# Seven products instead of eight in both MLP matrix products, by 2x2 blocks

## The chip, the cores and the metric

One core of a Trainium2 chip runs the whole program. The metric is the device time of the program in microseconds (us). TensorE (PE) multiplies, VectorE (DVE), ScalarE (ACT) and GpSimd (POOL) do the element-wise work, SyncE (SP) issues nearly all DMAs. Each engine takes its instructions in order and waits on semaphores.

## The reference

A trunk of one layer on 1024 tokens of 1024 channels, in fp32: an adaLN-conditioned mixer with four branches, gates and an output projection, and then the MLP that this change is about.

```python
def reference(x, c, positions, norm1_g, norm2_g, ada_w, ada_b, w_in, ..., w_out, mlp_w1, mlp_w2, final_g):
    ...
        h = rmsnorm(x, norm2_g[l]) * (1.0 + scale2) + shift2
        x = x + gate2 * (jnp.square(jax.nn.relu(h @ mlp_w1[l])) @ mlp_w2[l])
    return rmsnorm(x, final_g)
```

`mlp_w1` is 1024 x 4096, `mlp_w2` 4096 x 1024. `rmsnorm` divides by the root of the mean square over the channels.

## The kernel before

Activations lie transposed, channels on the 128 partitions and tokens along the free axis, in two halves of 512 tokens (`hf` 0 and 1). Each fp32 product is made of three: `split` (L109, L110) casts a matrix to `hi` on ACT and subtracts on DVE, `lo = raw - hi`; `mm3` (L125) issues hi·hi, hi·lo and lo·hi as matmuls of 128x128 by 128x512 into one PSUM bank. Weights come as blocks `raw` of 512 KB and are split as they arrive.

`outproj` makes `x1` half by half: eight channel blocks, each 24 matmuls, the residual on DVE (L1039), the square on ACT and the sum of squares `ssq`. `rstd` sums `ssq` over the partitions with a matmul by ones (`one`, L1065), takes the root on ACT (L185) and four reciprocals on DVE (L187). `norm_block` (L175 to L177) then makes `gh`, `gl`, the split input of the MLP.

`mlp` runs over 16 groups of 256 hidden channels. In a group, `up` makes four blocks (two channel blocks, two halves) of 24 matmuls each, applies relu on ACT (L1094) and the square on DVE (L1095), and splits the result into `aa`; `down` multiplies it into all eight output blocks, six matmuls each, and adds each to `x1` on DVE (L1107). Hidden activations and `x1` stay in SBUF. The first up products need the first half's norm only. The last two groups are written out in another order, with the last quarter in 256-column pieces, so that the final norm (L1119 to L1122) of earlier tokens is made beside the matmuls of later ones.

A scheduler orders the recorded program for each engine; pools (`wp`, `bp`, `pb`) decide which tiles share memory, and so some of the waits.

Of the kernel before, what the change touches and what calls it, by code (L numbers as in the profile page):

```python
# [9 lines left out]
FP32 = mybir.dt.float32  # L10
FR = mybir.dt.float32r
# [4 lines left out]
P = 128  # L16
# [47 lines left out]
def layout(x, c, positions, norm1_g, norm2_g, ada_w, ada_b, w_in, dn_conv_w, dn_a_log,  # L64
# [19 lines left out]
    o["w2"] = ct(A["mlp_w2"][0].reshape(32, P, 1024))  # L84
# [13 lines left out]
class Trunk:  # L98
# [45 lines left out]
    def cond_rows(self, pool):  # L144
        """Silu of the condition, the same row on all partitions."""
# [43 lines left out]
    def start(self):  # L189
        nc, A = self.nc, self.A  # L190
        cp = self.cp
        self.cst = cp.tile([P, NCST], FP32, name="cst")
# [251 lines left out]
    def rsqrt(self, x, y, t):  # L444
        """y = x ** -0.5 by Newton's iteration."""
# [17 lines left out]
    def dn_scalars(self):  # L463
        """Generator: beta, the decays and their logs per token, [token, head, chunk]."""
# [31 lines left out]
    def dn_proj(self, s, h):  # L496
        """Projection s of q, k, v of head h: its generator, the taps on DVE, the Silu."""
# [55 lines left out]
    def dn_mix(self, h, q, kT, vT, Es):  # L553
# [61 lines left out]
        # the 32-blocks on the diagonal for the inverse: partition = column group * 32 + block * 8 + chunk  # L615
# [8 lines left out]
    def dn_inverse(self, s):  # L624
        """Generator: the inverses of the 32-blocks by substitution, then back to the blocks' places."""
# [28 lines left out]
    def dn_levels(self, s):  # L654
        """The inverse of the 128-blocks out of that of the 32-blocks, doubled twice; transposed in TT."""
# [22 lines left out]
    def dn_scan(self, h, s):  # L678
# [44 lines left out]
        # rms norm with the norm of q folded in  # L723
# [129 lines left out]
    def mixers(self):  # L853
        """DeltaNet and retention: the projections of later heads fill the waits of the chains."""
# [83 lines left out]
    def branches(self, order, ahead=3):  # L938
        nc, A, bp = self.nc, self.A, self.pb
        blk = lambda w, n, o=0: [w[:, (o + k) * P:(o + k + 1) * P] for k in range(n)]  # L940
        self.acc = [bp.tile([P, NB, 512], FP32, tag="acc", name="acc", bufs=2) for _ in range(2)]
# [7 lines left out]
        def load_y(br):  # L949
            yh = bp.tile([P, 4, T], FR, tag="y", name="yh", bufs=2)  # L950
            yl = bp.tile([P, 4, T], FR, tag="y", name="yl", bufs=2)
# [65 lines left out]
    def outproj(self):  # L1017
# [5 lines left out]
        self.x1, self.gh, self.gl = [None] * 2, [None] * 2, [None] * 2  # L1023
        rs = [None, None]

        def h2(hf, k):
            self.norm_block(self.x1[hf][:, k], rs[hf], self.a2[:, k:k + 1], self.modc[:, 24 + k:25 + k],
                            self.gh[hf][:, k], self.gl[hf][:, k], bp, "t2k", 4)
        for hf in range(2):
            x1 = self.x1[hf] = bp.tile([P, NB, 512], FP32, tag="acc", name="x1", bufs=2)  # L1030
            ssq = bp.tile([P, 512], FP32, tag="ssq", name="ssq", bufs=1)
            for db in range(NB):
# [7 lines left out]
                                               op0=ALU.mult, op1=ALU.add)  # L1040
                self.sumsq(x1[:, db], ssq, db, nc.vector if db == NB - 1 else nc.gpsimd)
                if hf == 1 and db > 0:
                    h2(0, db - 1)
            if hf == 1:
                h2(0, NB - 1)
# [25 lines left out]
    def mlp(self):  # L1071
        nc, A, bp = self.nc, self.A, self.pb
        blk = lambda w: [w[:, k * P:(k + 1) * P] for k in range(NB)]
        NG = 16

        def load2(g):
            w2 = []
            for fb in range(2):
                raw = self.wp.tile([P, 1024], FP32, tag="raw", name="raw", bufs=2)
                nc.sync.dma_start(out=raw, in_=A["w2"][2 * g + fb])  # L1080
                bh = bp.tile([P, 1024], FR, tag="bh", name="bh", bufs=2)
                bl = bp.tile([P, 1024], FR, tag="bl", name="bl", bufs=2)
                self.split(raw, bh, bl)
                w2.append((bh, bl))
            return w2

        def up(aa, w, fb, hf, o=0, n=512):
            wh, wl = w
            sl = slice(hf * 512 + o, hf * 512 + o + n)
            ps = self.psm()[:, :n]  # L1090
            self.mm3(ps, blk(wh), blk(wl), [self.gh[hf][:, k, o:o + n] for k in range(NB)],
# [137 lines left out]
```

## Time and profile before

| | before |
|---|---|
| runs | 2035.49, 2041.83, 2037.52 us |
| median | 2037.52 us |
| profiled execution: span | 2034.8 us |
| TensorE busy | 1972.2 us, 97% |
| DVE, ACT, POOL busy | 54%, 28%, 9% |
| mean granted clock of TensorE | 0.993 |

The span is that of one profiled execution, from its first to its last instruction; the median of the runs is 2.7 us longer. Busy shares are means over stages that differ much, so the stage of the change has windows of its own below.

### The profile page before, as it was taken

The page shows a single profiled execution, that of the slowest core. Times are in us where ns is not written, and L with a number is a line of the kernel's source. Part 1 is how long each engine was busy: PE and PEld are TensorE (multiplying, and loading weights), DVE is VectorE, ACT ScalarE, POOL GpSimd, SP SyncE. Part 2 cuts the span into 40 slices and gives each one's busy share as a digit, 9 for nine tenths or more (in the row PEclk, how much of TensorE's full clock was granted, in tenths as well). Part 3 has the DMA queues.
Part 4 walks back from the last instruction along what each step waited for, and adds up shares of the span by engine and source line. Part 5 has one row for each costly group of instructions (what it writes and reads, how often), then busy time and mean ns, then how long its engine had stood idle before and what let it go on. Part 6 is the DMA issues. An engine that isn't in the chain of part 4 may idle for free.

```text
span 2034.8 us, 23666 instructions
## 1 busy us (share of the span) xinstructions
PE 1972.2 (97%) x9460; PEld 1629.6 (80%) x9460; DVE 1096.4 (54%) x1947; ACT 566.6 (28%) x922; POOL 187.6 (9%) x151
## 2 busy tenths in 40 slices
PE   5999989999999999999999999999999999999997
PEld 3888867777888888788788788878888888888886
DVE  7755679776744461352522224774455544455567
ACT  4524534332212231211212123432211222211133
POOL 4101211010000000011111112200000000000001
PEclk9999999999999999999999999999999999999999
DMA  7322121132222271251511213321111111111122
GB/s 280 128 84 84 54 54 43 43 75 72 63 73 63 78 237 48 92 167 52 163 55 45 90 42 104 124 73 46 48 52 42 42 63 51 43 52 42 42 83 93
DMA packets 89178, 162.10 MB, mean 80 GB/s; under 512 B 39014, under 2 KB 41702, under 8 KB 89068
## 3 DMA queue, kind: packets, MB, share of 16 engines
q1 hardware_dynamic: 87788, 156.40, 23.8%
q0 software_dynamic: 1280, 4.20, 0.9%
q8 instruction: 74, 1.21, 0.3%
q14 instruction: 36, 0.29, 0.0%
HBM read 142.20 MB, written 14.17 MB: 77 GB/s over the span
## 4 chain that ended last, share of the span: by engine, by line
PE 56%; DVE 1%; DMA 0%; ACT 0%; issue 0%; DVEq 0%; ACTq 0%
PE mm L125 55%; DMA yraw<-yd 0%; DVE x L1122 0%; DVE rs L187 0%; DVE yl L110 0%; PE sm L1065 0%; ACT whi L109 0%; DVE nt L175 0%; DVE x L1107 0%; DVE sig L996 0%; ACT rs L185 0%; ACT yh L109 0%; DVE ssq L1060 0%; DVE bl L110 0%; ACT sig L970 0%
## 5 line engine op out<-in xcount | busy, mean ns | idle before, releaser
L125 PE MATMUL mm<-aa,bh 128*128 128x512 f32 (+1 forms) x1056 | 317.3, 383 | 0.0
L110 DVE TENSOR_TENSOR wlo<-raw,whi 128x1024 fp32r<-128x1024 f32 x121 | 151.3, 1251 | 283.1 <-ACT whi L109 282.4
L1107 DVE SCALAR_TENSOR_TENSOR x<-mm,modc,x 128x512 f32<-128x512 f32 (+1 forms) x264 | 192.1, 734 | 109.8 <-PE mm L125 107.9
L109 ACT CAST whi<-raw 128x1024 fp32r<-128x1024 f32 x123 | 129.2, 1051 | 423.4 <-PE mm L125 293.5
L125 PEld LDWEIGHTS mm<-aa,bh 128*128 128x128 f32 x1056 | 196.2, 188 | 39.0 <-DVE aa L110 0.3
L125 PE MATMUL mm<-hh,whi 128*128 128x512 f32 x560 | 218.3, 390 | 0.0
L125 PE MATMUL mm<-hh,wlo 128*128 128x512 f32 x560 | 218.0, 389 | 0.0
L125 PE MATMUL mm<-hl,whi 128*128 128x512 f32 x560 | 217.9, 389 | 0.0
L415 PE MATMUL mm<-hh,wlo 128*128 128x512 f32 x512 | 205.7, 402 | 0.0
L415 PE MATMUL mm<-hh,whi 128*128 128x512 f32 x512 | 205.5, 401 | 0.0
L415 PE MATMUL mm<-hl,whi 128*128 128x512 f32 x512 | 204.5, 399 | 0.0
L125 PE MATMUL mm<-aa,bl 128*128 128x512 f32 (+1 forms) x528 | 202.0, 383 | 0.0
L125 PE MATMUL mm<-gh,whi 128*128 128x512 f32 (+1 forms) x520 | 201.2, 388 | 0.0
L125 PE MATMUL mm<-gl,whi 128*128 128x512 f32 (+1 forms) x520 | 200.7, 386 | 0.5 <-DVE gl L177 0.5
L125 PE MATMUL mm<-gh,wlo 128*128 128x512 f32 (+1 forms) x520 | 200.6, 386 | 0.0
L109 ACT CAST bh<-raw 128x1024 fp32r<-128x1024 f32 x50 | 51.0, 1049 | 282.3 <-PE mm L125 275.3
L125 PEld LDWEIGHTS mm<-hh,whi 128*128 128x128 f32 x560 | 105.1, 188 | 22.4 <-issue 0.8
L125 PEld LDWEIGHTS mm<-hh,wlo 128*128 128x128 f32 x560 | 105.1, 188 | 22.0
L125 PEld LDWEIGHTS mm<-hl,whi 128*128 128x128 f32 x560 | 105.1, 188 | 21.5
L125 PEld LDWEIGHTS mm<-aa,bl 128*128 128x128 f32 x528 | 99.2, 188 | 19.3
L125 PEld LDWEIGHTS mm<-gl,whi 128*128 128x128 f32 x520 | 97.7, 188 | 21.1 <-DVE gl L177 0.9
L125 PEld LDWEIGHTS mm<-gh,whi 128*128 128x128 f32 x520 | 97.6, 188 | 20.4 <-issue 0.5
(308 smaller groups left out, 3154.6 us busy)
## 6 DMA issues: line engine op xcount, KB each, us to landing
raw<-in_wt SPq DMA_DIRECT2D x80, 512.0 KB, 3.5
raw<-in_w SPq DMA_DIRECT2D x69, 512.0 KB, 4.3
adaw<-in_ada SPq DMA_DIRECT2D x64, 256.0 KB, 3.9
adaw<-in_ada SPq DMA_DIRECT2D x16, 512.0 KB, 7.0
raw<-in_wbr SPq DMA_DIRECT2D x16, 512.0 KB, 4.0
yraw<-yd SPq DMA_DIRECT2D x32, 256.0 KB, 3.3
raw<-in_wo SPq DMA_DIRECT2D x16, 512.0 KB, 3.7
xt<-in_xT SPq DMA_DIRECT2D x16, 256.0 KB, 4.8
```

Source lines behind the costliest of these rows:

```text
L109: nc.scalar.copy(out=hi, in_=raw)
L110: (eng or nc.vector).tensor_tensor(out=lo, in0=raw, in1=hi.bitcast(FP32), op=ALU.subtract)
L125: self.nc.tensor.matmul(out=ps, lhsT=a, rhs=b, start=(i == 0), stop=(i == 3 * n - 1))
L415: self.nc.tensor.matmul(out=ps, lhsT=blk(a, k), rhs=r[hf][:, k], start=(k == 0 and i == 0), stop=(k == NB - 1 and i == 2))
L1107: nc.vector.scalar_tensor_tensor(out=x, in0=ps[:, :tn], scalar=self.modc[:, 40 + db:41 + db], in1=x, op0=ALU.mult, op1=ALU.add)
```

## The change

Each of the two products is cut into 2x2 blocks. For the up product a *pair* is two blocks of 128 hidden channels, by two halves of 512 input channels, by the two halves of tokens; for the down product (four *chunks* `c` of 1024 hidden channels, in each four pairs `m`) it is two blocks of output channels by two halves of the chunk's hidden channels. A pair takes seven products of half the contraction, 12 matmuls each, 84 in all, where four full ones take 96. In return sums of blocks are needed. Of the weights: s3 = a11 + a21 and s1 = a21 + a22 on DVE, s2 = s1 + a11 and s4 = s2 + a12 on POOL (the stored blocks carry signs). Of the activations: `t3`, `n2`, `n1`, `t4` beside `b11`, `b21`, `b22`. Of the results: the product banks are combined; bank `a` is copied out by ACT while TensorE goes on to accumulate in it.

`h2_first` and `h2_rest` make the up operands. The first two products of five pairs, which need the first token half alone, are done *early* (L1149 to L1160), while the second half is normalized. The up stage stores seven operand blocks per pair to DRAM (`ad`, 112 stores of 256 KB); `load` (L1233 to L1239) brings 28 tiles per chunk back through seven `st` tiles, casts them on ACT and subtracts on DVE (`put`, L1054, L1055), for each operand right after the product of the chunk's last pair that reads the old one. `x1` is stored by `outproj` and loaded again ahead of the down stage. The final norm of both halves stands behind the last product; no piece has 256 columns any more. Pools are laid out anew; memory of `wp` and `pb` goes to the MLP's pool `pm`.

```diff
-    o["w2"] = ct(A["mlp_w2"][0].reshape(32, P, 1024))
+    o["w2"] = ct(A["mlp_w2"][0].reshape(4, 4, 2, P, NB, P).transpose(0, 4, 3, 2, 1, 5).reshape(4, NB, P, 1024))
...
-            rs[hf] = self.rstd(ssq)
-            pool, tag, nbuf = (bp, "y", 2) if hf == 0 else (self.bp, "h", 4)
-            self.gh[hf] = pool.tile([P, NB, 512], FR, tag=tag, name="gh", bufs=nbuf)
-            self.gl[hf] = pool.tile([P, NB, 512], FR, tag=tag, name="gl", bufs=nbuf)
-        for k in range(NB):
-            h2(1, k)
+                if hf == 1:
+                    self.h2_first(db, rs)
+            ps = self.pss()
+            nc.tensor.matmul(out=ps, lhsT=self.one, rhs=ssq, start=True, stop=True)
+            if hf == 0:
+                rs = bp.tile([P, 512], FP32, tag="rs", name="rs", bufs=2)
+                self.rms(ps, rs)
+                self.S = {"b11": self.opset(self.xb, "b16"), "b21": self.opset(self.xb, "b16")}
+        self.ps_rs = ps
...
+    def put(self, op, k, x):
+        hi, lo = self.S[op][:, 0, k], self.S[op][:, 1, k]
+        self.nc.scalar.copy(out=hi, in_=x)
+        self.nc.vector.tensor_tensor(out=lo, in0=x, in1=hi.bitcast(FP32), op=ALU.subtract)
...
+    def h2_rest(self, k, rs):
+        nc = self.nc
+        self.h2_raw(1, k, rs, nc.vector)
+        self.h2_raw(1, k + 4, rs, nc.gpsimd)
+        x11, x21, x12, x22 = self.x1[0][:, k], self.x1[0][:, k + 4], self.x1[1][:, k], self.x1[1][:, k + 4]
+        tt = lambda eng, o, a, b: eng.tensor_tensor(out=o, in0=a, in1=b, op=ALU.subtract)
+        neg = lambda o, a, b: nc.vector.scalar_tensor_tensor(out=o, in0=a, scalar=-1.0, in1=b, op0=ALU.mult,
+                                                             op1=ALU.subtract)
+        n2 = self.st("n2")
+        tt(nc.vector, x11, x11, x12)
+        neg(n2, x22, x11)
+        self.put("n2", k, n2)
+        tt(nc.gpsimd, x12, x22, x12)
+        self.put("t3", k, x12)
+        self.put("n1", k, x11)
+        neg(x21, n2, x21)
+        self.put("t4", k, x21)
...
+        def sums():
+            s = {n: pm.tile([P, 512], FP32, tag="sg", name=n, bufs=4) for n in ("s3", "s1", "s2", "s4")}
+            add = lambda eng, o, a, b: eng.tensor_tensor(out=o, in0=a, in1=b, op=ALU.add)
+            add(nc.vector, s["s3"], a11, a21)
+            add(nc.vector, s["s1"], a21, a22)
+            add(nc.gpsimd, s["s2"], s["s1"], a11)
+            add(nc.gpsimd, s["s4"], s["s2"], a12)
+            src.update(s)
+        def get(n):
+            if n[0] == "s" and n not in src:
+                sums()
+            hi = pm.tile([P, 512], FR, tag="wh", name="wh", bufs=7)
+            lo = pm.tile([P, 512], FR, tag="wl", name="wl", bufs=7)
+            self.split(src[n], hi, lo)
+            return hi, lo
...
+    def product(self, ps, w, op, start):
+        wh, wl = w
+        n = 0
+        for k in range(4):
+            sl = slice(k * P, (k + 1) * P)
+            rh, rl = self.S[op][:, 0, k], self.S[op][:, 1, k]
+            for a, b in ((wh[:, sl], rh), (wh[:, sl], rl), (wl[:, sl], rh)):
+                self.nc.tensor.matmul(out=ps, lhsT=a, rhs=b, start=start and n == 0, stop=(n == 11),
+                                      skip_group_check=True)
+                n += 1
...
+        rs = self.st("rs")
+        self.rms(self.ps_rs, rs)
+        for o in ("n2", "t3", "n1", "t4"):
+            self.S[o] = self.opset(self.bp, "h")
+        early = pm.tile([P, 8, 512], FP32, tag="ex", name="early", bufs=1)
+        for p in range(NE):
+            w = self.wpair_first(A["w1"][2 * p])
+            a, b = self.bank(), self.bank()
+            self.product(a, w[0], "b11", True)
+            nc.scalar.copy(out=early[:, p], in_=a)
+            self.product(b, w[1], "b21", True)
+            x = self.st("x11")
+            tt(nc.vector, x, b, early[:, p], ALU.add)
+            sq(x, x)
+            store("b11", p, x)
+            if p > 0:
+                self.h2_rest(p - 1, rs)
+        self.S["b22"] = self.opset(self.xb, "b16")
+        for k in range(4):
+            self.put("b22", k, self.x1[1][:, k + 4])
+        sums = self.xb.tile([P, 8, 512], FP32, tag="b16", name="sums", bufs=4)
+        ns = [0]
+        def fresh():
+            ns[0] += 1
+            return sums[:, ns[0] % 8]
+        def up(p, after):
+            e = p < NE
+            get = self.wpair(A["w1"][2 * p], A["w1"][2 * p + 1])
+            a, c = self.bank(), self.bank()
+            def prod(ps, w, o, start):
+                self.product(ps, get(w), o, start)
+                after(o)
+            if e:
+                v1 = early[:, p]
+                x11 = self.st("x11")
+                nc.sync.dma_start(out=x11, in_=ad["b11", p])
+            else:
+                prod(a, "a11", "b11", True)
+                x11 = self.st("x11")
+                nc.scalar.copy(out=x11, in_=a)
+            prod(c, "s3", "t3", True)
+            x22 = self.st("x22")
+            nc.scalar.copy(out=x22, in_=c)
+            prod(a, "s2", "n2", e)
+            x21 = self.st("x21")
+            if e:
+                tt(nc.vector, x21, a, v1, ALU.add)
+                tt(nc.gpsimd, x22, x22, v1, ALU.add)
+                prod(c, "a22", "t4", False)
+                stt(x21, c, -1.0, x21, ALU.mult, ALU.subtract)
+            else:
+                nc.scalar.copy(out=x21, in_=a)
+                b = self.bank()
+                prod(b, "a12", "b21", True)
+                tt(nc.vector, x11, b, x11, ALU.add)
+                sq(x11, x11)
+                store("b11", p, x11)
+            prod(a, "s1", "n1", False)
+            stt(x22, a, -1.0, x22, ALU.mult, ALU.subtract)
+            if not e:
+                prod(c, "a22", "t4", False)
+                stt(x21, c, -1.0, x21, ALU.mult, ALU.subtract)
+            sq(x22, x22)
+            store("b22", p, x22)
+            sq(x21, x21)
+            store("b21", p, x21)
+            prod(a, "s4", "b22", False)
+            x12 = self.st("x12")
+            if e:
+                tt(nc.vector, x12, a, v1, ALU.add)
+                sq(x12, x12)
+            else:
+                nc.scalar.activation(out=x12, in_=a, func=AF.Relu)
+                tt(nc.vector, x12, x12, x12, ALU.mult)
+            n1, n2, t4 = fresh(), fresh(), fresh()
+            tt(nc.vector, n1, x11, x12, ALU.subtract)
+            store("n1", p, n1)
+            tt(nc.vector, x12, x22, x12, ALU.subtract)
+            store("t3", p, x12)
+            stt(n2, x22, -1.0, n1, ALU.mult, ALU.subtract)
+            store("n2", p, n2)
+            stt(t4, n2, -1.0, x21, ALU.mult, ALU.subtract)
+            store("t4", p, t4)
...
+        def load(c, o):
+            pool, tag = place.get(o, (self.bp, "h"))
+            self.S[o] = self.opset(pool, tag, 1 if tag == "ex" else 4)
+            for j in range(4):
+                r = self.st("ar")
+                nc.sync.dma_start(out=r, in_=ad[o, 4 * c + j])
+                self.put(o, j, r)
+        for p in range(NP):
+            up(p, (lambda o: load(0, o)) if p == NP - 1 else (lambda o: None))
+        x1 = [self.xb.tile([P, NB, 512], FP32, tag="b16", name="x1", bufs=4) for _ in range(2)]
+        for d in range(NB):
+            for hf in range(2):
+                nc.sync.dma_start(out=x1[hf][:, d], in_=self.x1d[hf][d])
...
+        def down(c, m, after):
+            get = self.wpair(A["w2"][c, 2 * m], A["w2"][c, 2 * m + 1])
+            d0, d1 = 2 * m, 2 * m + 1
+            g0, n1 = self.modc[:, 40 + d0:41 + d0], ng[:, d1:d1 + 1]
+            x11, x12, x21, x22 = x1[0][:, d0], x1[1][:, d0], x1[0][:, d1], x1[1][:, d1]
+            a, c_, b = self.bank(), self.bank(), self.bank()
+            last = c == 3
+            def prod(ps, w, o, start):
+                self.product(ps, get(w), o, start)
+                after(o)
+            def snap(ps, x, g):
+                v = self.st("v")
+                nc.scalar.activation(out=v, in_=ps, func=AF.Copy, scale=g)
+                tt(nc.gpsimd, x, x, v, ALU.add)
+            def add(ps, x, g):
+                stt(x, ps, g, x, ALU.mult, ALU.add)
+            prod(a, "a11", "b11", True)
+            snap(a, x11, g0)
+            prod(c_, "s3", "t3", True)
+            snap(c_, x22, n1)
+            prod(a, "s2", "n2", False)
+            snap(a, x21, n1)
+            prod(b, "a12", "b21", True)
+            add(b, x11, g0)
+            prod(a, "s1", "n1", False)
+            add(a, x22, n1)
+            prod(c_, "a22", "t4", False)
+            add(c_, x21, n1)
+            prod(a, "s4", "b22", False)
+            add(a, x12, g0)
+            if last:
+                for d, hf in ((d0, 0), (d1, 0), (d0, 1), (d1, 1)):
+                    square(d, hf)
+        for c in range(4):
+            for m in range(4):
+                down(c, m, (lambda o: load(c + 1, o)) if m == 3 and c < 3 else (lambda o: None))
```

Three places show what the change does to the engines' order. DVE where the output projection ends, before: `x_9779` is x1 of the second half, `nt` and `gl` its norm for the MLP.

```order
L1039 SCALAR_TENSOR_TENSOR x_9779<-mm,modc,xr 128x512
L110 TENSOR_TENSOR wlo<-raw,whi 128x1024
L110 TENSOR_TENSOR bl<-raw,bh 128x1024
L1060 TENSOR_TENSOR ssq<-ssq,sq 128x512
L187 RECIPROCAL rs<-rs 128x128 x4
L110 TENSOR_TENSOR bl<-raw,bh 128x1024
L175 SCALAR_TENSOR_TENSOR nt<-x_9779,a_9471,rs 128x512 x3
L177 SCALAR_TENSOR_TENSOR gl<-nt,modc,gh 128x512 x3
```

The same place after: `x_9810` is x1 of the second half, `x_9496` of the first, `wl` the low part of the first up weights.

```order
L1035 SCALAR_TENSOR_TENSOR x_9810<-mm,modc,xr 128x512 x2
L1342 TENSOR_TENSOR ssq<-ssq,sq 128x512
L187 RECIPROCAL rs<-rs 128x128 x4
L110 TENSOR_TENSOR wl<-raw,wh 128x512 x2
L1060 TENSOR_TENSOR x_9810<-x_9810,rs 128x512 x2
L110 TENSOR_TENSOR wl<-raw,wh 128x512 x2
L1073 TENSOR_TENSOR x_9496<-x_9496,x_9810 128x512 x2
L1060 TENSOR_TENSOR x_9810<-x_9810,rs 128x512 x2
```

The first weights' low parts now stand behind the reciprocals; before, the weights of the first up products were ready ahead of them. TensorE at the same place, after (before, the matmul `sm<-ssq,one` stood 18 matmuls deep in the up products, `gh` and `gl`):

```order
L125 MATMUL mm<-mh,wlo 128x512
L1042 MATMUL sm<-ssq,one 128x512
L1125 MATMUL mm<-op,wh 128x512 x2
L1125 MATMUL mm<-op,wl 128x512
L1125 MATMUL mm<-op,wh 128x512 x2
L1125 MATMUL mm<-op,wl 128x512
```

The sum over partitions now stands between the projection's last matmul and the first product. ACT from the up to the down stage, after; `op<-ar` are the casts of reloaded operands, `x_12940` is the last up pair's last block, `v` the copies of the first down pair's banks. Before, there is no such place.

```order
L1198 COPY x_12796<-mm 128x512
L1054 CAST op<-ar 128x512 x3
L109 CAST wh<-raw 128x512
L1054 CAST op<-ar 128x512
L109 CAST wh<-s_13000 128x512
L1054 CAST op<-ar 128x512 x12
L1219 ACTIVATE x_12940<-mm 128x512
L1054 CAST op<-ar 128x512 x3
L1282 ACTIVATE v<-sm,modc 128x512
L1282 ACTIVATE v<-mm,ng_12969 128x512
L1282 ACTIVATE v<-sm,ng_12969 128x512
```

All three copies `v` stand behind the last of the 28 casts.

## Rows read from the trace of the kernel before

**Rows 1.** the page's table of engines: busy us, share of the span, instructions
```profile
PE 1972.2 (97%) x9460; PEld 1629.6 (80%) x9460; DVE 1096.4 (54%) x1947; ACT 566.6 (28%) x922; POOL 187.6 (9%) x151
```

**Rows 2.** windows: PE, PEld, DVE, ACT, POOL busy; clock, DMA share, GB/s
```profile
1340.00:1440.00 100.00, 100.00 (x443) 82.61 (x442) 55.71 (x74) 23.73 (x34) 0.00 (x0) 1.00 0.15 53
1840.00:1940.00 100.00, 100.00 (x442) 82.79 (x442) 49.67 (x64) 21.27 (x29) 0.00 (x0) 1.00 0.15 48
```

**Rows 3.** chain that ended last: start us, length, engine, line, count
```profile
1333.15 650.10 PE mm L125 x2866
2029.12 2.12 DVE x L1122 x3
```

**Rows 4.** groups of TensorE in the MLP, 1319.9 to 2022: busy us, mean ns
```profile
L125 PE MATMUL mm<-aa,bh 128*128 128x512 f32 x992 | 305.5, 389 | 0.0
L125 PE MATMUL mm<-gh,whi 128*128 128x512 f32 x504 | 196.7, 391 | 0.0
L125 PE MATMUL mm<-aa,bl 128*128 128x512 f32 x496 | 192.9, 389 | 0.0
L125 PE MATMUL mm<-aa,bh 128*128 128x256 f32 x64 | 11.8, 286 | 0.0
```

**Rows 5.** timeline where outproj ends: start, length, engine, line
```profile
1319.68 0.39 PE L125 MATMUL mm<-mh,wlo 128*128 128x512 f32 x1
1319.91 0.39 PE L125 MATMUL mm<-gh,whi 128*128 128x512 f32 x1
1320.11 0.75 DVE L1039 SCALAR_TENSOR_TENSOR x<-mm,modc,xr 128x512 f32<-128x512 f32 x1 [3.21 <-PE mm L125]
1323.29 0.69 DVE L1060 TENSOR_TENSOR ssq<-ssq,sq 128x512 f32<-128x512 f32 x1
1324.12 1.10 PE L1065 MATMUL sm<-ssq,one 128*128 128x512 f32 x2
1325.25 0.69 ACT L185 ACTIVATE rs<-sm,eps 128x512 f32<-128x512 f32 x1 [2.80 <-PE sm L1065]
1325.98 3.39 DVE L187 RECIPROCAL rs<-rs 128x128 f32<-128x128 f32 x4 [2.00 <-ACT rs L185]
```

**Rows 6.** timeline: DVE in the MLP; DVE and POOL in the branches
```profile
1347.07 1.28 DVE L110 TENSOR_TENSOR aa<-r,aa 128x512 fp32r<-128x512 f32 x2
1348.27 2.07 DVE L1107 SCALAR_TENSOR_TENSOR x<-mm,modc,x 128x512 f32<-128x512 f32 x3
...
908.29 1.23 DVE L110 TENSOR_TENSOR wlo<-raw,whi 128x1024 fp32r<-128x1024 f32 x1 [5.59 <-ACT whi L109]
919.11 1.28 POOL L997 TENSOR_TENSOR acc<-acc,sig 128x512 f32<-128x512 f32 x1 [6.87 <-DVE sig L996]
919.13 2.34 DVE L110 TENSOR_TENSOR bl<-raw,bh 128x1024 fp32r<-128x1024 f32 x1
```

**Rows 7.** groups of ACT in the MLP
```profile
L109 ACT CAST aa<-r 128x512 fp32r<-128x512 f32 x61 | 37.9, 621 | 61.7 <-DVE r L1095 61.7
```

**Rows 8.** DMA: landing of raw blocks (512 KB) in the MLP; issues of yraw
```profile
DMA to landing us min/median/max: 4.1/4.4/5.5
yraw<-yd SPq DMA_DIRECT2D x32, 256.0 KB, 3.3
```

**Rows 9.** TensorE after a wait in the mixers: window with its clock, timeline
```profile
445.00:450.00 5.00, 5.00 (x30) 0.50 0.00 0
...
444.62 1.97 PE L662 MATMUL sm<-XX,N 64*64 64x64 f32 x16 [4.10 <-DVE XX L668]
447.53 0.63 PE L415 MATMUL mm<-hl,whi 128*128 128x512 f32 x1
```

**Rows 10.** timeline of the program's end
```profile
2020.60 0.28 PE L125 MATMUL mm<-aa,bl 128*128 128x256 f32 x1
...
2022.58 3.48 DVE L1122 SCALAR_TENSOR_TENSOR x<-x,prm,rs 128x256 f32<-128x256 f32 x5
2027.77 3.47 DVE L1122 SCALAR_TENSOR_TENSOR x<-x,prm,rs 128x256 f32<-128x256 f32 x5
```

More of the change, by code (lines that the diff above doesn't have):

```diff
@@ L940, in branches @@
         blk = lambda w, n, o=0: [w[:, (o + k) * P:(o + k + 1) * P] for k in range(n)]
-        self.acc = [bp.tile([P, NB, 512], FP32, tag="acc", name="acc", bufs=2) for _ in range(2)]
+        self.acc = [self.xb.tile([P, NB, 512], FP32, tag="b16", name="acc", bufs=4) for _ in range(2)]
         self.mh, self.ml = [None, None], [None, None]
@@ new lines, in h2_first @@
+    def h2_first(self, k, rs):
+        self.h2_raw(0, k, rs, self.nc.vector)
+        self.put("b11" if k < 4 else "b21", k % 4, self.x1[0][:, k])
+    def h2_rest(self, k, rs):
[15 more added lines that the diff above has]
+        self.put("t4", k, x21)
@@ new lines, in st, with wpair @@
+    def st(self, name):
+        return self.pm.tile([P, 512], FP32, tag="st", name=name, bufs=7)
+    def wpair(self, s0, s1):
+        nc, pm = self.nc, self.pm
+        r = []
+        for s in (s0, s1):
+            r.append(pm.tile([P, 1024], FP32, tag="raw", name="raw", bufs=2))
+            nc.sync.dma_start(out=r[-1], in_=s)
+        a11, a12, a21, a22 = r[0][:, :512], r[0][:, 512:], r[1][:, :512], r[1][:, 512:]
+        src = {"a11": a11, "a12": a12, "a22": a22}
+        def sums():
[13 more added lines that the diff above has]
+            return hi, lo
+        return get
@@ new lines, in product, with bank @@
+    def product(self, ps, w, op, start):
[8 more added lines that the diff above has]
+                n += 1
+    def bank(self):
+        self.nbank = getattr(self, "nbank", 0) + 1
+        return self.psm() if self.nbank % 2 else self.pss()
@@ L1053, in sumsq, with wpair_first @@
+    def wpair_first(self, s):
+        r = self.pm.tile([P, 1024], FP32, tag="raw", name="raw", bufs=2)
+        self.nc.sync.dma_start(out=r, in_=s)
+        out = []
+        for i in range(2):
+            hi = self.pm.tile([P, 512], FR, tag="wh", name="wh", bufs=7)
+            lo = self.pm.tile([P, 512], FR, tag="wl", name="wl", bufs=7)
+            self.split(r[:, i * 512:(i + 1) * 512], hi, lo)
+            out.append((hi, lo))
+        return out
     def sumsq(self, x, ssq, i, eng):
@@ L1188, in build @@
         self.yd = [[dp.tile([P, T], FP32, name=f"yd{b}_{h}") for h in range(4)] for b in range(4)]
[L1189 to L1194 removed]
+        right = ExitStack()
+        self.wp = right.enter_context(tc.tile_pool(name="wp", bufs=1, side="right"))
+        with tc.tile_pool(name="cq", bufs=1, side="right") as self.cq:
+            s4 = ExitStack()
+            self.s4 = s4.enter_context(tc.tile_pool(name="s4", bufs=1, reuse_waits="tile"))
+            self.start()
+            with tc.tile_pool(name="sp", bufs=1, reuse_waits="tile") as sp:
                 self.pooling(sp)
[L1196 removed]
                 self.spatial(sp)
[L1198 to L1201 removed]
+            s4.close()
+            with tc.tile_pool(name="mp", bufs=1, reuse_waits="tile") as mp:
+                self.mp = mp
                 self.mixers()
[L1203 to L1206 removed]
+        self.xb = ctx.enter_context(tc.tile_pool(name="xb", bufs=1, reuse_waits="tile"))
+        self.pb = right.enter_context(tc.tile_pool(name="pb", bufs=1, side="right", reuse_waits="tile"))
+        self.branches((1, 2, 0, 3))
+        self.outproj()
+        right.close()
+        with tc.tile_pool(name="pm", bufs=1, side="right", reuse_waits="tile") as self.pm:
             self.mlp()
[L1208 to L1211 removed]
 def kernel(**inputs):
```

190 lines of the change are left out of this document (57 added, 133 removed).

## The prediction

> **What bounds the kernel now.** I read the page's engine table first: TensorE is busy 1972.2 of 2034.8 us [rows 1]. Then the windows over the MLP, because an average over a long program says nothing about one stage: six windows of 100 us each show TensorE at 100.00 with 442 or 443 matmuls, VectorE (DVE) near half and GpSimd (POOL) at nothing, at full granted clock, 2.4 GHz [rows 2]. So a 512-column matmul costs 100/443 = 0.226 us of TensorE here, and TensorE alone sets the pace. The chain says the same: one stretch of 2866 matmuls, 650.10 us long, with a handful of DVE rows behind it [rows 3]. The groups give the counts: 992 + 3 x 504 + 496 = 3000 matmuls of 512 columns, and 64 + 32 + 48 = 144 of 256 columns [rows 4]. The first MLP matmul starts at 1319.91 directly behind the output projection's last (1319.68) [rows 5]; the last one ends at 2020.88 [rows 10]. The stage is 701.0 us without a hole, and 13.9 us of norm and output follow to 2034.8.
>
> **The change, term by term.** All terms are against the profiled 2034.8 us; the median of the runs, 2037.52, is 2.7 above it and is added at the end.
>
> *TensorE's own work.* 32 pairs x 7 products x 12 matmuls = 2688, all of 512 columns: 2688 x 0.226 = 607.5 us. Against 701.0 that is **-93.5**. This is certain; everything else is what the rest costs.
>
> *The price of DVE work beside POOL.* Two DVE operations in a row on 128x512 take 1.28, three from PSUM 2.07, so about 0.60 and 0.66 each when queued [rows 6]. The MLP before has no POOL operation. After, it has about 135 (block sums, additions to x1, squares), and the trace shows elsewhere what that does: a 128x1024 DVE subtraction takes 1.23 alone and 2.34 when it starts just behind a POOL addition of 1.28 [rows 6]. Each POOL operation therefore takes about 1.1 us from a DVE that has work with two SBUF operands queued. The Trainium skill, "SBUF — State Buffer", section "SBUF: two separate sides", says that the loser of the port shared by DVE and GpSimd is blocked for the whole instruction; the row agrees, with 1.1 of 1.28. DVE's MLP work is some 690 operations, 690 x 0.62 = 428 us, plus at most 135 x 1.1 = 148: 576 of TensorE's 607. On average it fits; where work bunches it doesn't, and these are the places:
>
> *(a) Start.* Before, the second half's norm runs beside the first half's up products; the first matmul that needs it is far behind. Now the first product's split `wl` stands behind the four reciprocals on DVE. From the rows: last projection matmul 1320.1, x 0.75, square 0.6, ssq 0.69, sum over partitions 1.10, square root 0.69, reciprocals 3.39, one `wl` 0.68 [rows 5]: TensorE idles about 8.4 less the few matmuls that need only `wh`. **+8**.
>
> *(b) First s3.* After 120 early matmuls (27.1 us) the product s3·t3 waits for a `wl` that is the 55th DVE operation behind the reciprocals: 55 x 0.62 = 34, with nine POOL operations up to 44. That leaves 8 to 17; I take **+14**, nearer to the POOL row, because DVE is never idle in this stretch.
>
> *(c) Pairs.* An early pair has 60 matmuls (13.6 us) and 18 DVE plus 3 POOL operations: 18 x 0.62 + 3.3 = 14.5. So 0 to 2 us each; **+4** for five. The other pairs have 84 matmuls (19.0 us) against 20 x 0.62 + 2.2 = 14.6 (up) and 13 x 0.62 + 5.5 = 13.6 (down): covered. Their tight spot is the bank `a`: ACT must copy it between two products that are one product (2.7 us) apart, and the third product's copy (x21) stands in ACT's queue behind the cast of the next pair's s2. Counted from the end of the pair before: the raw block is freed 1.2 before it and lands at 3.4 (0.2 to issue, 4.4 [rows 8]); six DVE operations bring s1 at 7.6; s2 on POOL 8.9; its cast 9.5, the copy 10.2 with the hand-overs; needed at 10.8, after four products. 0.6 us is left. 0 to 12 over 22 pairs; **+5**.
>
> *(d) Up to down.* In pair 15, 28 operand tiles are reloaded through seven `st` tiles that the epilogue shares: landing 3.3 [rows 8], cast 0.62 [rows 7], subtraction 0.6, with the queues some 5.2 us per turn; with about four tiles free 28 x 5.2/4 = 36 us. ACT's copy `v` of the first down bank stands behind all 28 casts, and the third down product needs that bank about 25 us after the casts begin: 11 short, and 3 to 6 more before the seventh, which waits for additions of x1 on POOL. 11 to 17; **+14**.
>
> *(e) Three chunk changes.* The same reload without an epilogue. From the first product's end in the last pair to the seventh's start in the next are twelve products, 32.5 us. In it DVE has 28 subtractions, 7 bank additions and about 15 weight operations: 50 x 0.62 = 31, and eight POOL operations bring it to 38. 3 to 6.5 each; **+14** for three.
>
> *(f) Tail.* Before, half the tokens' norm is under TensorE and the last quarter has two reciprocals. After, both halves follow the last product: three sums over partitions (3.3 [rows 5]), the root 0.7, then on DVE eight reciprocals (6.8), ten multiplications (6.6), and 3.6 for the last output, as now from 2031.2 to 2034.8: 21.0 if POOL's six multiplications cost nothing, 25.4 with four of them in DVE's way (before, five multiplications of only 256 columns took 3.47 with POOL beside them [rows 10]). Against 13.9 that is 7 to 11.5; I take **+11**, since both engines work on the same half at once.
>
> *(g) Clock.* After 4.10 us idle the granted clock was 0.50 for 5 us, which is 1.2 GHz, and 512-column matmuls took 0.63 instead of 0.39 [rows 9]. Such a stretch loses about 2 us. Where DVE is the one that is late it costs nothing further; I take two, **+4**. The Trainium skill, "TensorE: Matmul & The Clock Gate", "Part 1: The HAM clock gate", has the array throttled whenever it has idled and speaks against opening holes in a full stream; if the three chunk changes also counted, by this row's 2 us each, the sum would be 6 higher.
>
> Upstream of the MLP TensorE's order is the same; the stores of x1 (16) and of the activations (112) go through SP and nobody waits for them at once. Sum: -93.5 + 8 + 14 + 4 + 5 + 14 + 14 + 11 + 4 = -19.5, a span of 2015.3, with 2.7: **2018**.
>
> **Rivals.**
> *Covers hold.* Every term at its low end: 8 + 8 + 0 + 0 + 11 + 9 + 7 + 2 = 45, so -48.5: 1989; with only (a) and (f) left, at 8 and 11, 1963. For it: DVE was half idle [rows 2], and DVE operations on PSUM have one SBUF operand. Against: the 2.34 row.
> *Weights land late (no change).* One pair's raw blocks are freed only by the pair before, so each load has little lead. At the row's largest landing, 5.5, the spot in (c) is 0.5 late: 27 x 0.5 = 14, of which 5 are in the sum: 2027. At 5.9 it is 0.9 late in each: 2037. For it: stores and loads now triple the traffic. Against: the stage has DMA share 0.15 now.
> *DVE becomes the bound (slower).* If DVE and POOL alternate all the way, with 576 us of work and in-order waits between, each pair is held by its DVE queue. From 0.7 us per pair on (19.5/27) the gain is gone; at 1.2 it is 2018 + 32 = 2050. For it: the 576. Against: the full pairs have 4 us of DVE slack each.
>
> **How the numbers follow.** My sum 0.58 (own range 2004 to 2031), covers hold 0.17, late weights 0.12, DVE bound 0.13. A measurement tells 0.3%, 6.1 us, from no change: faster is below 2031.4, slower above 2043.6. Nearly all of the first and all of the second case is faster, 0.72; late weights and the upper edge of my sum are the same, 0.15; slower 0.13. The range leaves out the far ends of the first and last rivals: 1984 to 2043.
>
> **What would show it.** Right: 2688 matmuls at 0.226 apart; a hole of about 8 us ahead of the first product, released by DVE `wl`; one of 8 to 17 ahead of the first s3; waits for ACT `v` at the first down pair and for DVE at each chunk change; pairs in between at 19.0 us; 21 to 25 us behind the last product; DVE operations of 1.7 us beside POOL. Wrong: pairs clearly over 19 us (DVE or weights), or holes (b), (d), (e) far off their ranges.

## The result: slower by 1.4%

| | before | after |
|---|---|---|
| median of 4 runs each | 2037.57 us | 2065.56 us |
| lowest to highest | 2035.49 to 2041.83 | 2062.21 to 2066.87 |
| profiled span | 2034.8 us | 2064.3 us |
| last projection matmul starts | 1319.68 | 1341.57 |
| from there to the end | 715.1 us | 722.7 us |
| from the last product's end to the end | 13.9 us | 27.2 us |

The ratio is 1.0137 [1.0121, 1.0153]. The forecast was 2018 us with 1984 to 2043 as its range, so the time lies outside it, on the other side of no change. The MLP stage with its tail came out 7.6 us longer than before, where 19.5 less were forecast, and 21.9 us are lost *ahead* of it, where TensorE executes the same matmuls in the same order.

The page's table of engines after, against [rows 1]:

```profile
PE 1945.1 (94%) x9004; PEld 1566.4 (76%) x9004; DVE 1226.4 (59%) x2132; ACT 689.0 (33%) x1177; POOL 402.1 (19%) x283
```

456 matmuls fewer took only 27 us off TensorE's busy time. Windows of TensorE alone (busy, matmuls, granted clock, DMA share, GB/s), first upstream in the mixers' branches, then among the full up pairs, after:

```profile
1000.00:1100.00 100.00, 98.94 (x426) 1.00 0.33 111
1490.00:1590.00 100.00, 100.00 (x432) 1.00 0.45 149
```

The same windows before:

```profile
1000.00:1100.00 100.00, 100.00 (x443) 1.00 0.26 85
1490.00:1590.00 100.00, 100.00 (x443) 1.00 0.16 52
```

The clock is at its upper level, 2.4 GHz, in all of them and TensorE is full. So a matmul itself has become dearer: 100/432 = 0.231 us by the count and not the 0.226 of [rows 2]. Taken from the start times of neighbouring 512-column matmuls, the mean spacing upstream is 227.10 ns before and 232.16 ns after; 4297 such intervals times 5.06 ns are 21.7 of the 21.9 us. Such a mean is what *spacing* stands for from here on.

The holes that the forecast was about are there too. Waits of TensorE in the MLP, after (in total, times, longest), and the timeline of its start, against [rows 5]:

```profile
PE sm L1125 <- ACT v L1282: 11.9, 3, 10.8
PE mm L1125 <- ACT v L1282: 8.2, 7, 2.5
PE sm L1125 <- ACT wh L109: 7.7, 1, 7.7
PE mm L1125 <- ACT wh L109: 6.9, 2, 4.7
PE mm L1125 <- DVE x L1138: 4.4, 4, 2.1
```

```profile
1344.42 1.10 PE L1042 MATMUL sm<-ssq,one 128*128 128x512 f32 x2 [2.45 <-DVE ssq L1342]
1346.27 3.39 DVE L187 RECIPROCAL rs<-rs 128x128 f32<-128x128 f32 x4 [2.00 <-ACT rs L185]
1347.78 1.22 PE L1125 MATMUL mm<-op,wh 128*128 128x512 f32 x2 [2.27 <-ACT wh L109]
1349.57 2.31 DVE L110 TENSOR_TENSOR wl<-raw,wh 128x512 fp32r<-128x512 f32 x2
1349.79 1.54 POOL L1060 TENSOR_TENSOR x<-x,rs 128x512 f32<-128x512 f32 x1 [10.45 <-DVE rs L187]
1350.26 0.79 PE L1125 MATMUL mm<-op,wl 128*128 128x512 f32 x1 [1.26 <-DVE wl L110]
1387.10 1.22 PE L1125 MATMUL sm<-op,wh 128*128 128x512 f32 x2 [7.67 <-ACT wh L109]
1392.98 0.80 PE L1125 MATMUL mm<-op,wh 128*128 128x512 f32 x1 [4.66 <-ACT wh L109]
```

One sees the chain of term (a), sums, reciprocals, `wl`; then the hole at the first s3 in two pieces, 7.67 us ahead of its first matmul and 4.66 behind its second, where a matmul with s2, a sum made on POOL, stands next in TensorE's order; and the copies `v` of the first down pair, with one wait of 10.8. The end of the chain that ended last, against [rows 3] and [rows 10]:

```profile
2037.03 0.86 PE sm L1265 x2
2037.89 1.73 PE sm L1266 x4
2039.70 0.70 ACT rs L185
2040.42 4.20 DVE rs L187 x5
2044.62 5.81 DVE x L1138 x5
2050.43 2.50 DVE rs L187 x3
2052.95 0.75 DVE x L1138
2053.70 1.67 DVEq L1390
2055.37 3.99 DVE x L1138 x3
```

### The profile page after: what moved, and what is told of

Read it like the earlier page. It is cut to its first block, busy times and chain, and to the rows that moved or that the text cites. A ratio compares the mean times of both kernels' runs of the same rounds, so it can differ in the third digit from the quotient of the medians.

```text
span 2064.3 us, 24238 instructions
## 1 busy us (share of the span) xinstructions
PE 1945.1 (94%) x9004; PEld 1566.4 (76%) x9004; DVE 1226.4 (59%) x2132; ACT 689.0 (33%) x1177; POOL 402.1 (19%) x283
## 3 DMA queue, kind: packets, MB, share of 16 engines
q8 instruction: 70, 1.15, 0.2%
## 5 line engine op out<-in xcount | busy, mean ns | idle before, releaser
L1125 PE MATMUL mm<-op,wh 128*128 128x512 f32 x928 | 298.1, 403 | 23.7 <-ACT v L1282 8.2
L1125 PE MATMUL sm<-op,wh 128*128 128x512 f32 x864 | 276.1, 400 | 22.8 <-ACT v L1282 11.9
L1125 PEld LDWEIGHTS mm<-op,wh 128*128 128x128 f32 x928 | 176.7, 192 | 72.9 <-ACT v L1282 12.4
L1125 PEld LDWEIGHTS sm<-op,wh 128*128 128x128 f32 x864 | 164.1, 191 | 64.7 <-ACT v L1282 14.0
L1125 PE MATMUL mm<-op,wl 128*128 128x512 f32 x464 | 185.2, 400 | 1.3 <-DVE wl L110 1.3
L1125 PE MATMUL sm<-op,wl 128*128 128x512 f32 x432 | 172.2, 399 | 0.0
L997 POOL TENSOR_TENSOR acc<-acc,sig 128x512 f32<-128x512 f32 x48 | 67.0, 1396 | 530.7 <-DVE sig L996 523.1
L1102 POOL TENSOR_TENSOR s<-s,raw 128x512 f32<-128x512 f32 x64 | 97.6, 1525 | 326.0 <-DVE s L1102 293.4
L109 ACT CAST wh<-s 128x512 fp32r<-128x512 f32 x128 | 79.3, 620 | 214.8 <-PE sm L1125 68.1
L110 DVE TENSOR_TENSOR wl<-s,wh 128x512 fp32r<-128x512 f32 x128 | 113.0, 883 | 54.5 <-ACT wh L109 53.7
L125 PEld LDWEIGHTS mm<-hl,whi 128*128 128x128 f32 x560 | 105.5, 188 | 24.2
```

Source lines behind the costliest of these rows:

```text
L109: nc.scalar.copy(out=hi, in_=raw)
L110: (eng or nc.vector).tensor_tensor(out=lo, in0=raw, in1=hi.bitcast(FP32), op=ALU.subtract)
L125: self.nc.tensor.matmul(out=ps, lhsT=a, rhs=b, start=(i == 0), stop=(i == 3 * n - 1))
L997: nc.gpsimd.tensor_tensor(out=a, in0=a, in1=sg, op=ALU.add)
L1102: add = lambda eng, o, a, b: eng.tensor_tensor(out=o, in0=a, in1=b, op=ALU.add)
L1125: self.nc.tensor.matmul(out=ps, lhsT=a, rhs=b, start=start and n == 0, stop=(n == 11), skip_group_check=True)
```

## Experiments

### Where do 22 us upstream go?

The change moves the pool of the weights: `wp` now lies at the upper end of SBUF (`side="right"`), the streamed operands at the lower. The addresses in the compiled programs show what that does. Before, weights (`whi`, `wlo`, `bh`, `bl`) and operands (`hh`, `hl`, `mh`, `ml`, `gh`, `aa`) all start at 1472 modulo 2048 bytes of their partition. After, operands start at 608 (`b22` of the down stage, one operand set of seven, at 2016) and the weights of the projections and the MLP at 2016, those of the branches at 1952. The first theory was that the operands' own start matters (1472 is a multiple of 64, 608 is not); its rivals were the place of the weights and the extra traffic.

```diff
+        self.pad = cp.tile([P, 8], FP32, name="pad")
```

The pad stands in the constants' pool, ahead of everything on the lower side: 32 bytes of it in before, 64 in the second run, 32 in after in the third. The fourth run pads after's `wp` and `pm` by 32 bytes as well, which moves the weights down, those of the branches included.

> The kernel before with 32 bytes of unused memory added to the pool of constants, so that nearly all matmul operands start 32 bytes past a multiple of 64; nothing else changes. Theory A (addresses): the start of the operands within 64 bytes sets the spacing of matmuls, 0.227 us at 0 and about 0.233 at 32. Then some 8200 matmuls lose up to 0.0065 us each: plus 30 to 50 us, 2068 to 2088. Theory B (traffic: stores, loads, DVE and POOL at work beside the matmuls made them slower): nothing changes, 2037. Theory C (any other layout, by accident of banks): unknown, and the next run with 64 bytes moves as well.

> The same with 64 bytes, so that the operands lie elsewhere but again at multiples of 64. Theory A: 2037, spacing 0.227. Theory B: 2037. Theory C (any shift matters): moves as the run with 32 bytes does.

> The changed kernel with 32 bytes added to the pool of constants alone: the streamed operands start at multiples of 64, the weights stay 32 past. Theory A, if the streamed operand decides: spacing back to 0.227, upstream -22, MLP -17, so 2026. If the weights decide: 2065. Theory B: 2065.

> The changed kernel with both the streamed operands and the weights at multiples of 64 (32 bytes added to the pool of constants and to two pools of the other side). Theory A: the output projection ends at 1320 as before instead of 1342, products are 2.72 us instead of 2.80, 2026 in all (2020 to 2032). Theory B: 2065.

Measured: 2039.49 us, ratio 0.9999 [0.9979, 1.0019], and 2040.13, 0.9996 [0.9975, 1.0017], for before moved by 32 and by 64 bytes, both at a spacing of 226.67 ns in the window from 1000 to 1100 us, with weights and operands moved together. After with only the operands moved: 2075.12, 1.0169 [1.0139, 1.0199], spacing 233.7 ns. After with both moved: 2066.8, 1.0122 [1.0089, 1.0156], 232.2 upstream. So the operands' own alignment is not it: that theory falls. Before keeps its spacing as long as weights and operands move together; after's changes where one moves *against* the other. The next kernel has nothing but matmuls, none of the reference's work: weights and one streamed operand in SBUF, moved against each other.

```diff
+    for s in SHIFTS:
+        run(R, 8192 + s)
+    for s in (0, 8, 40, 160):
+        run(H, s)
```

`run` issues 96 matmuls of 128x128 by 128x512 as the products do; `s` counts columns of 4 bytes, `R` holds operand and weights, `H` weights at the upper end of SBUF.

> Only matmuls, 96 in a row for each case (the order hi hi, hi lo, lo hi of the kernel), no other engine or transfer beside them; it computes nothing of the reference. The streamed operand lies still, the weights are moved by 0 to 1408 bytes behind it, and in four cases lie at the top of SBUF. Theory D (the place of the weights against the streamed operand sets the spacing): 227 ns at some shifts, 231 to 236 at others. Theory B (traffic of other engines and transfers): 227 ns in every case.

Groups of that kernel, 96 matmuls each: `cab` at shift 0, `cag` at 160 bytes, `caj` at 256, `cap` at 1024; `cat` at the upper end of SBUF, at an address that is the operand's modulo 256.

```profile
L49 PE MATMUL cag<-R 128*128 128x512 f32 x96 | 22.6, 395 | 0.0
L49 PE MATMUL cap<-R 128*128 128x512 f32 x96 | 21.9, 389 | 0.0
L49 PE MATMUL cab<-R 128*128 128x512 f32 x96 | 21.9, 389 | 0.0
L49 PE MATMUL caj<-R 128*128 128x512 f32 x96 | 21.9, 389 | 0.0
L49 PE MATMUL cat<-R,H 128*128 128x512 f32 x96 | 21.9, 389 | 0.0
```

Spacing by shift, worked out from the start times without the first eleven matmuls of each group (behind a slow group, a fast one takes up to seven matmuls to reach its pace):

```
bytes    0      32     64     96     128    160    192    224    256    384    512    640    672    704    1024   1408
ns     226.67 233.33 233.33 234.29 232.38 233.33 228.88 233.33 226.67 232.38 226.67 232.38 233.33 228.88 226.67 232.38
```

With weights at the upper end: 226.67 at the one shift that is congruent, 232.38 to 234.29 at three others. The reading: where weights and streamed operand start at the same address modulo 256 bytes (*congruent* from here on), the matmul stream runs at 226.67 ns; otherwise at 228.9 to 234.3. In this stretch no other engine works and the DMA share is 0.00, so traffic is no part of it. After, weights minus operands are 2016 - 608 = 1408, which is 128 modulo 256; the row says 232.38, the kernel has 232.2. The third run is at 96 (234.29 against 233.7), the fourth at 64 (233.33; 233.05 in the MLP, and 232.2 upstream, where the branches' weights are congruent: in their groups of 12 between slow ones the first matmuls still take 228 to 236 ns, the last 225 to 227). The Trainium skill, "SBUF — State Buffer", section "SBUF: two separate sides", has TensorE's port never waiting on anyone. These runs agree in so far as no other engine is needed for the loss; they show that it hangs on TensorE's own two addresses, and not by which mechanism.

If that is the cause, before must become slow by it alone, and after fast. Three edits, one kernel each: in before a pad behind the weights of `wp`, so that they are 128 bytes off; in before the pool `wp` at the upper end; in after 384 bytes ahead of the operands, since 1408 - 384 = 1024.

```diff
+            self.wp.tile([P, 32], FP32, name="pad")
...
-        self.wp = ctx.enter_context(tc.tile_pool(name="wp", bufs=1))
+        self.wp = ctx.enter_context(tc.tile_pool(name="wp", bufs=1, side="right"))
...
+        self.pad = cp.tile([P, 96], FP32, name="pad")
```

> The kernel before with 128 unused bytes behind its weights, so that the streamed operands start 128 bytes, and not 0, past the weights when counted in 2048 bytes. Theory D: spacing 231 to 235 ns, 2060 to 2085 us. Theory B, and theory E (the weights' place at the top of SBUF, far from the streamed operands): 227 ns, 2037.

> The kernel before with the pool of weights at the top of SBUF, as in the changed kernel; counted in 2048 bytes the streamed operands are now 544 bytes before the weights. Theories D and E: 231 to 235 ns, 2060 to 2085 us. Theory B: 227 ns, 2037.

> The changed kernel with 384 unused bytes among the constants, so that weights and streamed operands start alike when counted in 1024 bytes. Theory D, if the period is 1024 or less: 227 ns, the output projection ends at 1320, 2025 us. Theory E and theory B: 232 ns, 2065.

Before with its weights 128 bytes off took 2070.6 us in its one run, with them at the top, 544 bytes off, 2067.94: with all eight products, before is as slow as after. Its spacings are 231.5 and 231.9 upstream, 229.7 and 229.9 in the MLP. The MLP loses less because the weights of the down product, `bh` and `bl`, lie in `pb` and moved together with their operand `aa`. In the first run the up product is at 232.4 ns and the down product at 227.0, in the second at 233.3 and 226.8, within one stage of one kernel. The window of the first, where before held 443, and two of its groups in the MLP (in before 391 and 389 ns, [rows 4]):

```profile
1000.00:1100.00 100.00, 98.86 (x427) 1.00 0.35 111
L125 PE MATMUL mm<-gh,whi 128*128 128x512 f32 x498 | 197.1, 396 | 0.0
L125 PE MATMUL mm<-aa,bh 128*128 128x512 f32 x992 | 305.7, 389 | 0.0
```

After with 384 bytes of padding took 2041.35 us, 0.9997 [0.9977, 1.0016]: 24.2 us less than after's median, and no different from before; against before, measured beside each, after's 1.0137 has become 0.9997. Call this kernel *aligned*. Its windows:

```profile
1000.00:1100.00 100.00, 99.86 (x439) 1.00 0.32 103
1490.00:1590.00 100.00, 100.00 (x442) 1.00 0.47 151
```

So the addresses cost some 24 us, and without that cost the seven products come out even with the eight: no gain, where 19.5 us were forecast. (In this kernel only the branches' weights are still off, by 192 bytes modulo 256; their spacing is 229.15.) All that follows is measured on aligned versions, for they alone have the 0.226 of the forecast.

### What do the stalls cost, and what is POOL's part?

The next runs align the branches' weights too (a pad of 192 bytes in `pb`); that alone was not run, and upstream it is worth 1.7 us by the spacing (227.04 and not 227.44). The first moves every GpSimd operation of the MLP, the final norm's multiplications among them, to DVE; the second has eight early pairs, so 192 matmuls and not 120 ahead of the first s3; the third both; the fourth puts 36 matmuls, whose result is overwritten, ahead of the first s3.

```diff
-            add(nc.gpsimd, s["s2"], s["s1"], a11)
+            add(nc.vector, s["s2"], s["s1"], a11)
...
-                tt(nc.gpsimd, x, x, v, ALU.add)
+                tt(nc.vector, x, x, v, ALU.add)
...
-        NP, NE = 16, 5
+        NP, NE = 16, 8
...
-            if p > 0:
+            if 0 < p < 5:
...
+            if p == 0:
+                for i in range(36):
+                    nc.tensor.matmul(out=c, lhsT=w[1][0][:, (i % 4) * P:(i % 4 + 1) * P], rhs=self.S["b21"][:, 0, i % 4],
```

> The changed kernel with all tiles that TensorE reads starting alike in 256 bytes (as e8, and the branch weights too), and every POOL operation of the MLP moved to DVE. Theory L (a POOL operation costs a busy DVE 1.1 us, more than the 0.62 that DVE needs for it itself): the wait ahead of the first s3 7 instead of 12, the early pairs' waits 3 instead of 6, the three chunk changes 7 instead of 14, the wait of the first down pair unchanged at 14 since ACT's casts set it: about 2026. Theory N (POOL works beside DVE at little cost): DVE gets 135 more operations, the same places wait longer, 2050 or more.

> As e8 with the branch weights aligned too, and eight early pairs instead of five: 72 more early matmuls, 16.3 us, ahead of the first s3. If the wait there is DVE's backlog behind the reciprocals: the early pairs add 12 DVE operations (7.4 us) to the backlog too, so the wait falls from 12 to about 3, but three more pairs of 13.6 us against 14.5 of DVE: minus 9 plus 3, 2035. If it is a wait for something else (weights, ACT): unchanged at 12, 2041.

> Both together. Theory L: no wait ahead of the first s3, 2020 to 2026, faster than the kernel before by more than 0.3%. Theory N: 2045 or more.

> As e8 with the branch weights aligned too, and 36 matmuls (8.2 us) whose result is overwritten put ahead of the first s3, where TensorE waits. If a wait of this length is what halves the clock: the matmuls behind it run at 0.227 and not at 0.43 us, 2 us less slow time there; the other waits are as before. If not: slow matmuls stay. In the time, 2 us of 2041, no more than runs differ.

*Without POOL*: 2021.05 us, 0.9914 [0.9885, 0.9943], faster than both kernels. From the last projection matmul to the end DVE now does 141 operations more, and yet is busy only 13.1 us longer (540.26 against 527.17). Groups of DVE in the aligned kernel with POOL:

```profile
L110 DVE TENSOR_TENSOR wl<-s,wh 128x512 fp32r<-128x512 f32 x128 | 116.1, 907 | 50.6 <-ACT wh L109 49.8
L1056 DVE TENSOR_TENSOR op<-ar,op 128x512 fp32r<-128x512 f32 x112 | 90.5, 848 | 10.7 <-ACT op L1055 9.9
L1139 DVE SCALAR_TENSOR_TENSOR x<-mm,ng,x 128x512 f32<-128x512 f32 x16 | 11.9, 747 | 10.4 <-PE mm L1126 10.4
```

and without:

```profile
L110 DVE TENSOR_TENSOR wl<-s,wh 128x512 fp32r<-128x512 f32 x128 | 87.4, 686 | 21.6 <-ACT wh L109 21.5
L1056 DVE TENSOR_TENSOR op<-ar,op 128x512 fp32r<-128x512 f32 x112 | 73.0, 688 | 8.3 <-ACT op L1055 7.9
L1139 DVE SCALAR_TENSOR_TENSOR x<-mm,ng,x 128x512 f32<-128x512 f32 x16 | 12.0, 749 | 11.7 <-PE mm L1126 11.7
```

Operations with two SBUF operands fall from 907 and 848 to 686 and 688 ns, those with one operand from PSUM (`mm`) stay. That fits the shared port of the Trainium skill's section named above, which names DVE operations with two SBUF inputs, and the traces agree. 141 operations at 0.69 are 97 us; DVE's busy time grew by 13.1, so a POOL operation had cost it 0.60 on average, and the dependent work besides waited 1.4 to 1.75 us for POOL's result where DVE's takes 0.69. From the last projection matmul to the first full pair the price is higher. Windows of DVE there, with POOL and without:

```profile
1328.08:1459.84 131.76, 116.69 (x154) 0.88 0.43 144
1322.48:1443.24 120.76, 109.30 (x178) 0.93 0.46 153
```

24 operations more in 7.4 us less: by the same sum each of the 25 POOL operations there had cost DVE 0.96 us. The run doesn't separate the port from the shorter chain. In the early pairs it is throughput: there DVE is busy 28.74 of the 30 us from 1425 on in the aligned kernel.

*Eight early pairs*: 2040.87, 1.0005 [0.9988, 1.0023], no change. The wait has moved. The first s3 now starts at 1389.80 without one; TensorE waits 6.84 us in the sixth early pair instead, whose `wl` (made from `raw`, not from a sum `s`) stands in DVE's queue behind the operands of the second token half. Behind it come holes of 1.2 to 3.5 us some 15 us apart:

```profile
1373.78 0.68 DVE L1056 TENSOR_TENSOR op<-n,op 128x512 fp32r<-128x512 f32 x1
1374.38 0.68 DVE L110 TENSOR_TENSOR wl<-raw,wh 128x512 fp32r<-128x512 f32 x1
1375.11 0.80 PE L1126 MATMUL sm<-op,wl 128*128 128x512 f32 x1 [6.84 <-DVE wl L110]
```

More matmuls ahead don't help, since what TensorE waits for is DVE's queue, and each early pair has a place in it too: up to the first full pair this kernel loses 35.2 us, the aligned one 36.3. *Both*: 2021.64, 0.992 [0.9894, 0.9946], the same as without POOL alone.

*36 matmuls in the hole*: 2037.55 in one run, within the spread. Of their 8.2 us, 6.0 lay in the hole: the first full pair starts 127.6 us behind the first product, against 125.4. `wl` was still 3.3 us late and the clock still fell:

```profile
1369.96 0.50 PE L1126 MATMUL sm<-op,wl 128*128 128x512 f32 x1 [3.35 <-DVE wl L110]
1370.29 0.69 PE L1126 MATMUL sm<-op,wh 128*128 128x512 f32 x2
1370.78 0.63 PE L1126 MATMUL sm<-op,wl 128*128 128x512 f32 x1
```

So DVE's queue sets that place; what the clock alone would give back there this run does not tell.

## Why the prediction was wrong, step by step

What TensorE lost in each stretch of the MLP beyond its matmuls at 226.67 ns, in us, cut at the same matmul in each kernel:

| stretch | forecast | after | aligned | aligned, no POOL |
|---|---|---|---|---|
| start, first s3, early pairs: (a), (b), part of (c) | 26 | 37.0 | 36.3 | 25.3 |
| ten full up pairs, of (c) | 5 | 4.8 | 0.1 | 0.0 |
| last up and first down pair: (d) | 14 | 18.2 | 17.5 | 14.7 |
| the other down pairs: (e) | 14 | 26.0 | 22.8 | 24.0 |
| tail beyond 13.9: (f) | 11 | 13.3 | 13.4 | 11.0 |
| half clock: (g) | 4 | in the rows above | in the rows above | in the rows above |
| sum | 74 | 99.3 | 90.1 | 75.0 |
| the matmuls, against 701.0 | -93.5 | -91.7 | -91.7 | -91.7 |
| net, from the last projection matmul | -19.5 | +7.6 | -1.6 | -16.7 |

**The step that failed** is the one that was called certain, "2688 x 0.226 = 607.5 us", together with "Upstream of the MLP TensorE's order is the same" at no cost. The duration came from a row of a kernel in which weights and operands happen to be congruent modulo 256 bytes; I carried it over to a kernel whose pools are "laid out anew", and for that edit the sum has no term at all. In the MLP it cost 9.3 us net (722.7 - 713.4; where DVE is late a slower matmul hides in the wait), upstream 21.7. Before made slow by 128 bytes and after made fast by 384 show it in both directions. That is 31 of the 49 us by which the profiled span exceeds the forecast's 2015.3; of the other 18, 16 are stalls beyond the forecast's 74, and 2 come from reckoning with 0.226 and not 0.2267. Of the remaining gap upstream between the aligned kernels and before (their last projection matmuls start at 1328.08, 1322.48, 1326.70, 1323.52 and 1319.73, before's at 1319.68) only 1.4 us in the first is spacing. Before moved by 64 bytes, with order and spacing unchanged, has that matmul at 1325.27, so one profiled run differs from another there by that much without the change.

**A second step was too small: the stalls, 74 for 90, and first (g), +4**. The waits came where they were forecast, but half clock follows more of them. In the aligned kernel about 13 us of matmuls at 1.2 GHz: 2.9 behind the first product, 2.1 and 3.0 in the early pairs, 1.7 each at 1691, 1759 and 1926. Windows of TensorE there:

```profile
1335.00:1340.00 5.00, 3.86 (x10) 0.50 0.09 29
1380.00:1385.00 5.00, 5.00 (x16) 0.63 0.38 123
1410.00:1415.00 5.00, 5.00 (x14) 0.56 0.52 198
```

The forecast knew a case behind 4.10 us idle [rows 9]. Here half clock also followed 2.78 us idle ahead of 1408.2, 2.01 ahead of 1925.9 and 1.90 ahead of 1758.6, while after 2.23 ahead of 1841.6, and after 2.67 in the run with 36 matmuls, the clock stayed at 1.00:

```profile
1758.63 0.81 PE L1126 MATMUL mm<-op,wh 128*128 128x512 f32 x2 [1.90 <-ACT v L1283]
1758.60:1762.60 4.00, 3.97 (x10) 0.57 0.74 212
1841.60 0.73 PE L1126 MATMUL mm<-op,wh 128*128 128x512 f32 x2 [2.23 <-ACT v L1283]
1841.60:1846.00 4.40, 4.40 (x19) 1.00 0.72 227
```

So the length of the one idle stretch does not tell whether the clock falls, and what does stays open. The alternative that the forecast put in a sentence by itself, chunk changes counting too, was nearer, 10 for 13. The Trainium skill, "TensorE: Matmul & The Clock Gate", "Part 1: The HAM clock gate", named there, pointed the right way.

The terms of the sum one by one, with holes counted from start to start:

- **(a)** is right: 8 forecast; in the aligned kernel the first product starts 6.3 behind the last projection matmul, and the first `wl` adds 1.5.
- **(b)**, 8 to 17 with +14: the two holes of the aligned kernel are 7.4 and 5.3, together 12.2 beyond the spacing.
- **(c)** early, +4: 6.4 in holes of over 0.9 us. With the half clock and short waits beside them the three make 36.3 against 26.
- **(c)** full pairs, +5: nothing. Ten pairs ran 839 intervals in 190.23 us, 226.7 ns each, with POOL, stores and raw loads around them; the bank `a` was copied in time every time, so the 0.6 us of slack was real.
- **(d)**: 14.4 us in three holes around the change of stage, the largest 11.4, behind `v`; and 11.7 remain without POOL, which fits the count of casts ahead of `v`, though no run takes the casts away.
- **(e)** is the other term of stalls that was too small: 14.1 in holes of over 0.9 us, spread over the chunks and not at three places, but 22.8 with half clock and short waits, and no better without POOL (24.0), where DVE has the additions itself. Eight of these ten holes end with ACT's copy `v`, where the forecast's signs had DVE. Its sum also has a slip: 31 and eight times 1.1 are 39.8 and not 38, or 7.3 us for each change and 22 for three. That this is near 22.8 is luck, for the holes are not at the changes alone and the loss does not shrink without POOL.
- **(f)**: 13.3 for 11. The eight reciprocals took 6.7 as counted and nine multiplications on the chain beside POOL's 10.6 (5.81 + 0.75 + 3.99); not counted were 1.7 of queue (`DVEq`) and 1.3 more behind the last multiplication, 4.9 for 3.6. Without POOL it is 11.0.

**The POOL row** [rows 6], 1.1 us of a busy DVE per POOL operation, decided more than the sum made of it. The sum took POOL's work as given and let the average fit (576 of 607). But up to the first full pair, where DVE is queued, a POOL operation took 0.96 us from DVE, more than the 0.69 that DVE needs to do it itself; over the whole MLP it took 0.60. DVE operations beside POOL reached 1.77 us, as forecast (the four norm multiplications, L1060).

**The rivals.** *Covers hold* is out: 90 us of stalls, not 45. *Weights land late* is out: the full pairs, where each load has least lead, lose nothing in the aligned kernel. *DVE becomes the bound* holds in the early pairs, not in the full up pairs, so not as it was put (a loss per pair all the way). None of the three had a matmul that takes longer.

## What to carry to other kernels

A duration read from a trace holds for the addresses that it was measured at: when a change lays out memory anew, compare the matmul spacing in a stretch that the change doesn't touch first, and compare start addresses of weights and streamed operands. Fewer matmuls are worth only what the elementwise work can cover where it bunches, at the start, at changes of stage and at the tail; here, once aligned, the 91.7 us of matmuls that were saved came back as 90 us of stalls. Helping a queued DVE with GpSimd additions can cost more than it brings (up to the first full pair here, 0.96 us of DVE where 0.69 was saved): count what DVE loses beside them.

## What the hardware showed that was not expected

A stream of 128x128 by 128x512 matmuls runs at 226.67 ns a matmul when weights and streamed operand start at the same address modulo 256 bytes, and at 228.9 to 234.3 otherwise, 1 to 3.4%, at full granted clock, 2.4 GHz, and with every other engine idle. Why the offsets 64 and 192, which are mirror images, differ (233.33 and 228.88) stays open. And the version with aligned weights and no GpSimd work, at 2021.05 us, is the one that beats both kernels, by 0.86% [0.57, 1.15] against before; of the forecast's -19.5 us in the stage it shows -16.7.
